# A hybrid decoder trunk on one core: the first load in three pieces, a shorter run of zero products, and the second row tile's products in another order

## Chip, core and metric

The kernel runs on one core of a Trainium2 chip. The metric is the device time of one execution, in microseconds (us). Before the change it is 1411.94 us, the median of three runs (1411.52 to 1412.18).

## What is computed

The reference is a two-layer decoder trunk over 512 tokens of width 1024, all in float32. Layer 0 mixes tokens with a Mamba-2 SSD mixer, layer 1 with HGRN2; each layer then has a layer norm, a squared-ReLU MLP of width 4096, a second layer norm and a gated per-layer input. The change touches only the very beginning, the input projection of the SSD mixer:

```python
def ssd_mixer(u, w_in, conv_w, conv_b, dt_bias, a_log, d_skip, norm_w, w_out):
    zxbcdt = u @ w_in                       # (512 x 1024) @ (1024 x 5152)
    z, xbc, dt = jnp.split(zxbcdt, [SSD_D_INNER, SSD_D_INNER + SSD_CONV_DIM], axis=-1)
    xbc = jax.nn.silu(causal_depthwise_conv(xbc, conv_w, conv_b))
...
def reference(...):
    for i in range(DEPTH):
        mix = ssd_mixer(x, ...) if i % 2 == 0 else hgrn2_mixer(x, ...)
        h = layer_norm(DEEPNORM_ALPHA * x + mix, ...)
        h = layer_norm(DEEPNORM_ALPHA * h + sq_relu_mlp(h, ...), ...)
        x = h + jax.nn.sigmoid(h @ ple_w_gate[i]) * (p[i] @ ple_w_proj[i])
```

## The kernel before

**Products in three parts.** A float32 matrix is taken as a sum of two float32r parts: `hi` is a cast of it (ScalarE, or VectorE in one place), `lo` is the matrix minus `hi` (VectorE). A product of two such matrices is three matmuls, `hi*hi`, `hi*lo` and `lo*hi`, the lines L120, L121 and L122 of the helper `mm3`. They accumulate in one bank of PSUM, [128 x 512].

**The first four columns of blocks.** The activations lie transposed, as eight row tiles of 128 model dimensions by 512 tokens. Each is sent together with the weight rows that meet it (4 blocks of 128 output channels, so also 128 x 512): eight DMAs of 512 KB, L161, one per row tile, issued by SyncE (SP) one after the other into eight slots. The DMA's semaphores are eight lanes used in turn, and a DMA waits until the last one on its lane has landed. For each row tile `k` ScalarE casts the tokens (L167; VectorE for `k = 0`) and the weights (L171), and VectorE makes the two `lo` parts (L168, L172); for `k = 0` the weights are cast in two halves of 256 columns. The four output banks (`py0`, `py1` and two called `pj`) collect the products over `k`:

```python
    with tc.high_priority(offset=FIRST):                                     # L149
        zero = nc.const_aps.tensor(0.0, (P, 1), F32)
        ps = bank(psm, "pm")
        for _ in range(4):
            nc.tensor.matmul(ps[:, :256], zero.to_broadcast([P, P]), zero.to_broadcast([P, 256]), start=True, stop=True)
...
        for k in range(8):
            nc.sync.dma_start(slots[k], a["xw"][k])                          # L161
...
        parts = [[v[:, k % 2, i * P : (i + 1) * P] for v in four[k // 2]] for i in range(4)]
        if k == 0:
            for n, (w, t) in enumerate(((0, x_s.h(k)), (0, x_s.l(k)), (1, x_s.h(k)))):
                for i, out in enumerate(first):
                    nc.tensor.matmul(out, parts[i][w], t, start=n == 0, stop=False)   # L749
        else:
            for i, out in enumerate(first):
                mm3(out, *parts[i], x_s.h(k), x_s.l(k), False, k == 7)
```

For `k = 0` the twelve products go by kind: `hi*hi` of all four banks, then `hi*lo`, then `lo*hi` (L749). From `k = 1` on they go by bank, with `mm3`. In front of everything stand four matmuls of zeros on TensorE, 256 columns each (L153); nothing reads what they write. After `k = 3` come 64 small matmuls for the step sizes (L738), which read all eight slots.

**What follows.** The other blocks of the projection come one at a time, 512 KB of weights each (`unit`, L106 DMA, L113 cast, L116 `lo`), into a bank `pj` with 24 matmuls. Each bank is then convolved over time: ScalarE starts `cv` (L797), VectorE adds three shifted terms (L800: 509, 510 and 511 elements), ScalarE applies SiLU. The scan works on pairs of heads in `core`: TensorE transposes (L859, tile `pt`), VectorE makes from it `xw` and `xdt` (L866, L867), TensorE forms the state products from `xw` (L871, tile `pm`) and the products inside the chunks from `xdt` (L906), VectorE carries the states (L879 to L882, tile `pv`), and TensorE applies them (L923). The decay factors `a` come back from DRAM (L855) and become `b` by VectorE (L888), an exponential on ScalarE (L891) and a product with `cbm` on VectorE (L892).

**What sets the order.** No order is written out by hand here. A list scheduler places the instructions of the whole program when it is built, by priorities and by its own idea of when each would be ready. A change of the first instructions can therefore shift rows that the diff does not name. Each engine then runs its own list strictly in order.

## Time and profile before

| what | value |
|---|---|
| runs before | 1411.52, 1411.94, 1412.18 us |
| the profiled execution | 1411.34 us |
| its span in the trace | 1409.6 us |
| TensorE matmul busy | 1404.3 us (100%) |
| VectorE busy | 1069.1 us (76%) |
| ScalarE busy | 763.6 us (54%) |
| DMA, mean over the span | 129 GB/s |

The profile is of one execution. PE is TensorE's matmuls and PEld its weight loads, DVE is VectorE, ACT is ScalarE, SPq is SyncE's queue. In a timeline a row begins with its start, its duration, the engine and the line; `out<-in` are the tiles; in square brackets stands how long the engine sat idle before it and what it waited for. The chain of waits follows the last instruction backwards, at each step to what released it. Matmuls are pipelined, so the spans of neighbours overlap by some 0.16 us; in the chain the overlap is taken off. Line numbers are those of the kernel before; in the changed kernel those behind L161 are higher by five.

### The profile page before, as it was taken

The page shows a single profiled execution, that of the slowest core. Times are in us where ns is not written, and L with a number is a line of the kernel's source. Part 1 is how long each engine was busy: PE and PEld are TensorE (multiplying, and loading weights), DVE is VectorE, ACT ScalarE, POOL GpSimd, SP SyncE. Part 2 cuts the span into 40 slices and gives each one's busy share as a digit, 9 for nine tenths or more (in the row PEclk, how much of TensorE's full clock was granted, in tenths as well). Part 3 has the DMA queues.
Part 4 walks back from the last instruction along what each step waited for, and adds up shares of the span by engine and source line. Part 5 has one row for each costly group of instructions (what it writes and reads, how often), then busy time and mean ns, then how long its engine had stood idle before and what let it go on. Part 6 is the DMA issues. An engine that isn't in the chain of part 4 may idle for free.

```text
span 1409.6 us, 20400 instructions
## 1 busy us (share of the span) xinstructions
PE 1404.3 (100%) x8001; PEld 1168.1 (83%) x8001; DVE 1069.1 (76%) x1778; ACT 763.6 (54%) x1156; POOL 45.8 (3%) x92
## 2 busy tenths in 40 slices
PE   9999999999999999999999999999999999999998
PEld 7888888888988888888888888888898888888887
DVE  7989688698977668677986577678785867667795
ACT  7766465573354444545555547655555454544573
POOL 0000000001000000000000000000100000000100
PEclk9999999999999999999999999999999999999999
DMA  8433333234433444345621421222443444444731
GB/s 313 135 117 120 106 120 110 85 100 156 141 113 127 157 131 152 129 142 178 209 90 49 134 91 61 76 87 96 150 135 105 147 137 148 144 137 159 202 106 60
DMA packets 50399, 181.69 MB, mean 129 GB/s; under 512 B 5632, under 2 KB 6400, under 8 KB 50176
## 3 DMA queue, kind: packets, MB, share of 16 engines
q1 hardware_dynamic: 38784, 138.45, 29.6%
q0 software_dynamic: 11520, 41.95, 9.2%
q8 instruction: 63, 1.03, 0.3%
q14 instruction: 32, 0.26, 0.1%
HBM read 177.16 MB, written 2.16 MB: 127 GB/s over the span
## 4 chain that ended last, share of the span: by engine, by line
PE 99%; DMA 0%; DVE 0%; issue 0%; DVEq 0%
PE pj L120 25%; PE pj L121 25%; PE pj L122 25%; PE py L120 5%; PE py L122 5%; PE py L121 5%; PE py L906 1%; PE pt L238 1%; PE py L1175 1%; PE pm L923 1%; PE pm L871 1%; PE py L1301 1%; PE pt L859 0%; PE py L1303 0%; PE py L1240 0%; PE py L832 0%
## 5 line engine op out<-in xcount | busy, mean ns | idle before, releaser
L113 ACT CAST whi<-raw 128x1024 fp32r<-128x1024 f32 x218 | 228.8, 1050 | 333.2 <-PE pj L121 243.6
L120 PE MATMUL pj<-b,whi 128*128 128x512 f32 (+1 forms) x990 | 378.6, 383 | 0.0
L122 PE MATMUL pj<-b,wlo 128*128 128x512 f32 (+1 forms) x990 | 376.8, 381 | 0.0
L121 PE MATMUL pj<-b,whi 128*128 128x512 f32 (+1 forms) x990 | 376.6, 381 | 0.0
L116 DVE TENSOR_TENSOR wlo<-raw,whi 128x1024 fp32r<-128x1024 f32 x218 | 265.4, 1221 | 129.4 <-ACT whi L113 128.2
L121 PEld LDWEIGHTS pj<-b,whi 128*128 128x128 f32 x990 | 186.4, 188 | 34.6 <-issue 0.9
L122 PEld LDWEIGHTS pj<-b,wlo 128*128 128x128 f32 x990 | 186.3, 188 | 34.5
L120 PEld LDWEIGHTS pj<-b,whi 128*128 128x128 f32 x990 | 186.1, 188 | 34.0
L122 PE MATMUL pj<-whi,b 128*128 128x512 f32 x520 | 204.1, 392 | 0.0
L120 PE MATMUL pj<-whi,b 128*128 128x512 f32 x508 | 202.1, 398 | 0.0
L121 PE MATMUL pj<-wlo,b 128*128 128x512 f32 x508 | 199.2, 392 | 0.0
L113 ACT CAST whi<-r 128x1024 fp32r<-128x1024 f32 x76 | 80.0, 1053 | 68.5 <-PE pj L122 39.4
L122 PEld LDWEIGHTS pj<-whi,b 128*128 128x128 f32 x520 | 97.7, 188 | 20.1
L120 PEld LDWEIGHTS pj<-whi,b 128*128 128x128 f32 x508 | 95.5, 188 | 19.1 <-ACT b L1322 0.3
L121 PEld LDWEIGHTS pj<-wlo,b 128*128 128x128 f32 x508 | 95.5, 188 | 18.7 <-issue 0.2
L116 DVE TENSOR_TENSOR wlo<-r,whi 128x1024 fp32r<-128x1024 f32 x76 | 92.5, 1220 | 19.6 <-ACT whi L113 19.1
L122 PE MATMUL py<-whi,b 128*128 128x512 f32 x260 | 101.3, 390 | 0.0
L121 PE MATMUL py<-wlo,b 128*128 128x512 f32 x248 | 96.6, 389 | 0.0
L120 PE MATMUL py<-whi,b 128*128 128x512 f32 x248 | 96.4, 390 | 0.0
L329 POOL DMA_DIRECT2D r<-in_w x64 | 34.0, 532 | 1098.8 <-DVE wlo L116 544.3
L122 PEld LDWEIGHTS py<-whi,b 128*128 128x128 f32 x260 | 48.8, 188 | 10.2
L800 DVE SCALAR_TENSOR_TENSOR cv<-pj,cst,cv 128x509 f32<-128x509 f32 (+2 forms) x66 | 48.9, 746 | 10.6 <-ACT cv L797 9.8
(368 smaller groups left out, 1943.5 us busy)
## 6 DMA issues: line engine op xcount, KB each, us to landing
raw<-in_w SPq DMA_DIRECT2D x112, 512.0 KB, 3.3
r<-in_w POOLq DMA_DIRECT2D x64, 512.0 KB, 3.8
raw<-in_wssd SPq DMA_DIRECT2D x36, 512.0 KB, 3.9
a<-csd SPq DMA_DIRECT2D x16, 512.0 KB, 4.1
raw<-in_wso SPq DMA_DIRECT2D x16, 512.0 KB, 3.3
raw<-in_whq SPq DMA_DIRECT2D x16, 512.0 KB, 3.4
raw<-in_wg SPq DMA_DIRECT2D x15, 512.0 KB, 4.0
raw<-in_whvg SPq DMA_DIRECT2D x14, 512.0 KB, 3.4
```

The costliest lines, as they stand in the source:

```text
L113: nc.scalar.copy(hi[:, :n], f)
L116: nc.vector.tensor_sub(lo[:, :n], f, f32(hi[:, :n]))
L120: nc.tensor.matmul(out, sh, mh, start=start, stop=False, **kw)
L121: nc.tensor.matmul(out, sh, ml, start=False, stop=False, **kw)
L122: return nc.tensor.matmul(out, sl, mh, start=False, stop=stop, **kw)
L238: nc.tensor.transpose(pt[:, j * P : (j + 1) * P], src[:, k * P : (k + 1) * P], ident)
L329: queue.dma_start(t[i][u], src)
L800: nc.vector.scalar_tensor_tensor(cv[:, d:], ps[:, : T - d], convw[:, i, k : k + 1], cv[:, d:], ALU.mult, ALU.add)
L871: nc.tensor.matmul(pst_[:, c * P : (c + 1) * P], btok[:, c, :], xw[:, c].rearrange("p h q -> p (h q)"), start=True, stop=True)
L906: mm = nc.tensor.matmul(yds[0][64 * r : 64 * r + 64, sl], xdt[:, 2 * c + r, :], m[:, r, sl], start=True, stop=True)
L923: mm = nc.tensor.matmul(yo[:, c * P : (c + 1) * P], pv[:, c - 1].rearrange("p h q -> p (h q)"), cm[:, c * P : (c + 1) * P], start=True, st ...
L1175: nc.tensor.matmul(pcs[r][bs, at : at + n], kk[r][:, ts], qs, start=True, stop=True)
```

## The change

The fourth matmul of zeros gets 128 columns in place of 256. The first of the eight loads is issued as three DMAs: the tokens (128 x 512), then the weights in two pieces of 128 x 256; the other seven stay as they are. The products of the second row tile (`k = 1`) go by kind, as those of the first do. Casts, subtractions and the number of products stay.

```diff
@@ -149,8 +149,8 @@
-        for _ in range(4):
-            nc.tensor.matmul(ps[:, :256], zero.to_broadcast([P, P]), zero.to_broadcast([P, 256]), start=True, stop=True)
+        for n in (256, 256, 256, P):
+            nc.tensor.matmul(ps[:, :n], zero.to_broadcast([P, P]), zero.to_broadcast([P, n]), start=True, stop=True)
@@ -158,7 +158,12 @@
         for k in range(8):
-            nc.sync.dma_start(slots[k], a["xw"][k])
+            if k == 0:
+                nc.sync.dma_start(slots[0][:, 0, :], a["xw"][0][:, 0, :])
+                for i in range(0, T, 256):
+                    nc.sync.dma_start(slots[0][:, 1, i : i + 256], a["xw"][0][:, 1, i : i + 256])
+            else:
+                nc.sync.dma_start(slots[k], a["xw"][k])
             if k == 3:
@@ -743,10 +748,10 @@
-        if k == 0:
+        if k < 2:
             for n, (w, t) in enumerate(((0, x_s.h(k)), (0, x_s.l(k)), (1, x_s.h(k)))):
                 for i, out in enumerate(first):
-                    nc.tensor.matmul(out, parts[i][w], t, start=n == 0, stop=False)
+                    nc.tensor.matmul(out, parts[i][w], t, start=k == n == 0, stop=False)
```

In the built program the lists of the engines differ at these places, and again in a stretch of the SSD mixer. Behind TensorE's row 310 of some 6290 its list is that of before, row for row. Three places matter.

TensorE, the products of the second row tile (`whi_109` and `wlo_110` its weights, `b_4` the high and `b_6` the low part of the tokens). Before:

```order
L120 MATMUL py_26_174<-b_4_105,whi_109 128x512
L121 MATMUL py_26_174<-b_6_107,whi_109 128x512
L122 MATMUL py_26_174<-b_4_105,wlo_110 128x512
L120 MATMUL py_27_175<-b_4_105,whi_109 128x512
L121 MATMUL py_27_175<-b_6_107,whi_109 128x512
L122 MATMUL py_27_175<-b_4_105,wlo_110 128x512
```

and in the changed kernel:

```order
L754 MATMUL py_26_176<-b_4_105,whi_109 128x512
L754 MATMUL py_27_177<-b_4_105,whi_109 128x512
L754 MATMUL pj_178<-b_4_105,whi_109 128x512
L754 MATMUL pj_179<-b_4_105,whi_109 128x512
L754 MATMUL py_26_176<-b_6_107,whi_109 128x512
L754 MATMUL py_27_177<-b_6_107,whi_109 128x512
L754 MATMUL pj_178<-b_6_107,whi_109 128x512
L754 MATMUL pj_179<-b_6_107,whi_109 128x512
L754 MATMUL py_26_176<-b_4_105,wlo_110 128x512
```

The first product that reads the low weights was the third and is now the ninth.

VectorE, between the convolution of the seventh block (`cv_525` from bank `pj_493`, later `cv_527` from `pj_495`) and the second pair's `xw`. `wlo_759` and `wlo_797` (later `wlo_761`, `wlo_799`) are the low weights of the eleventh and twelfth block; TensorE is in the eighth at that time. Before:

```order
L931 TENSOR_TENSOR ecs_485<-pm_488,ecs_485 128x384
L892 TENSOR_TENSOR b_474<-b_474,cbm_448 128x1024
L888 TENSOR_SCALAR b_588<-a_565,toks_400 128x128 x4
L116 TENSOR_TENSOR wlo_759<-raw_755,whi_757 128x1024
L800 SCALAR_TENSOR_TENSOR cv_525<-pj_493,cst_165,cv_525 128x509
L116 TENSOR_TENSOR wlo_797<-raw_793,whi_795 128x1024
L800 SCALAR_TENSOR_TENSOR cv_525<-pj_493,cst_165,cv_525 128x510
L892 TENSOR_TENSOR b_588<-b_588,cbm_448 128x1024
L800 SCALAR_TENSOR_TENSOR cv_525<-pj_493,cst_165,cv_525 128x511
L866 TENSOR_TENSOR xw_573<-pt_567,toks_400 128x384
```

and in the changed kernel:

```order
L893 TENSOR_SCALAR b_590<-a_567,toks_402 128x128 x5
L805 SCALAR_TENSOR_TENSOR cv_527<-pj_495,cst_167,cv_527 128x509
L936 TENSOR_TENSOR ecs_487<-pm_490,ecs_487 128x384
L805 SCALAR_TENSOR_TENSOR cv_527<-pj_495,cst_167,cv_527 128x510
L897 TENSOR_TENSOR b_590<-b_590,cbm_450 128x1024
L805 SCALAR_TENSOR_TENSOR cv_527<-pj_495,cst_167,cv_527 128x511
L116 TENSOR_TENSOR wlo_761<-raw_757,whi_759 128x1024
L116 TENSOR_TENSOR wlo_799<-raw_795,whi_797 128x1024
L871 TENSOR_TENSOR xw_575<-pt_569,toks_402 128x384
```

Both low-weight subtractions now stand behind the whole convolution; the subtraction `wlo_759` stood ahead of it. `ecs` has moved from ahead of the convolution into it, and the product of `b_474` and `cbm` has moved further ahead.

TensorE, between the transposes `pt` of the second pair and its state products `pm`, which read `xw`. Before:

```order
L859 MATMUL pt_567<-cst_165,xs_389 128x128 x4
L120 MATMUL pj_640<-b_4_105,whi_643 128x512
L121 MATMUL pj_640<-b_6_107,whi_643 128x512
L122 MATMUL pj_640<-b_4_105,wlo_645 128x512
L120 MATMUL pj_640<-b_4_105,whi_643 128x512
L871 MATMUL pm_576<-xw_573,btok_441 128x128 x3
```

and in the changed kernel:

```order
L864 MATMUL pt_569<-cst_167,xs_391 128x128 x4
L120 MATMUL pj_642<-b_4_105,whi_645 128x512
L121 MATMUL pj_642<-b_6_107,whi_645 128x512
L122 MATMUL pj_642<-b_4_105,wlo_647 128x512
L120 MATMUL pj_642<-b_4_105,whi_645 128x512
L121 MATMUL pj_642<-b_6_107,whi_645 128x512
L876 MATMUL pm_578<-xw_575,btok_443 128x128 x3
```

One product more lies between the two.

## Prediction

> **What bounds the kernel now.** I read the chain of waits first, whole and then stretch by stretch, since the page gives TensorE 100% of the span and the question is only what delays TensorE.
>
> ```profile
> PE 99%; DMA 0%; DVE 0%; issue 0%; DVEq 0%
> 0.74 3.40 DMA acc<-in_xw
> 4.17 0.44 DVE b L167
> 4.61 0.14 issue
> 4.74 0.70 PE py L749 x2
> ...
> 1405.12 0.43 DVE sg L456
> ```
>
> From 4.74 us to the last rows on VectorE the chain never leaves TensorE; its 40-us pieces show no other engine. So a product that starts earlier at 4.74 brings the end forward by as much, unless a wait opens on TensorE afterwards, and a wait that opens anywhere costs its full length. That leaves two questions: when the first product starts, and whether the places where the order of VectorE and TensorE has changed open a wait.
>
> Next I read the timeline of the first 5 us.
>
> ```profile
> 0.74 1.80 SPq L161 DMA_DIRECT2D acc<-in_xw  x4
> 0.78 3.36 PE L153 MATMUL pm<-const-float32-0.0 128*128 128x256 f32 x8 [0.78 <-PEq L1452]
> 4.17 0.71 ACT L171 CAST whi<-acc 128x256 fp32r<-128x256 f32 x2 [2.15 <-DMA acc<-in_xw]
> 4.71 0.30 PEld L749 LDWEIGHTS py<-b,whi 128*128 128x128 f32 x2 [0.98 <-ACT whi L171]
> 4.74 0.70 PE L749 MATMUL py<-b,whi 128*128 128x512 f32 x2 [0.61 <-DVE b L167]
> ```
>
> The first tile lands 3.40 us after its issue, at 4.14. Then two things run side by side: VectorE's cast of the tokens (0.44 and 0.14 to the product) and ScalarE's first half of the weights, from 4.17 to the weight load at 4.71, 0.54. Both end within 0.03 us of each other. The zeros keep TensorE until 0.78 + 3.36 = 4.14, so they hold up nothing.
>
> **Term 1, the first load.** The DMA engines move this rate while the first tile arrives (last number of the first row, GB/s; third from its end, 1.00, is the granted clock), and these are the landings of the step weights and of the first four tiles:
>
> ```profile
> 3.50:3.75 0.25, 0.25 (x2) 0.23 (x1) 0.00 (x0) 0.00 (x0) 0.00 (x0) 1.00 1.00 410
> raw<-in_wdt SPq DMA_DIRECT2D x1, 128.0 KB, 6.3
> DMA to landing us min/median/max: 3.4/4.9/6.5
> 2.58 0.58 SPq L164 DMA_DIRECT2D raw<-in_wdt  x1
> ```
>
> At 410 GB/s the tokens' 262 KB take 0.64 us and a piece of weights, 131 KB, 0.32. If the three pieces follow each other at that rate, the last lands at 4.14 as now, the first weights at 4.14 - 0.32 = 3.82, the tokens at 3.50. Small pieces need not lose rate: the step weights, 128 KB in rows as short as those of a piece, were issued at 2.58 and landed 6.3 later, at 8.9; the fourth tile, issued last of four from 0.74 (four issues in 1.80, so 0.45 each, the last at 2.09), landed up to 6.5 later, at 8.6. That is 0.3 us for 128 KB. The weight load then comes 0.03 + 0.54 = 0.57 after 3.82, at 4.39, the product at 4.42; by the tokens it could come at 3.50 + 0.03 + 0.44 + 0.14 = 4.11, which does not decide. The second weight half is cast from 4.21 (0.71 / 2 = 0.36 each), is ready at 4.57 + 0.14 = 4.71, and the third product wants it about 0.5 after 4.42, at 4.9. **Gain 0.32.** The bounds: if the weights came with the tokens, 4.74 - 4.11 = 0.63 gained. If a piece needs from its own issue as long as a whole tile, 3.40, the first weights, issued second at 1.19, land at 4.59 and the product starts at 5.19, 0.45 lost. I take 0.32, since the step weights are the nearest row in size and kind and moved at the full rate.
>
> The Trainium skill, DMA: Bandwidth & Descriptors, section Bandwidth, speaks against cutting a load: it wants at least 1 MiB per DMA for 75% of peak. Here the trace disagrees: 128 KB behind a full queue took 0.3 us, some 0.43 TB/s.
>
> **Term 2, the zeros.** Eight passes take 3.36, so 0.42 each; the change removes half a matmul, one such pass, and the zeros end at 3.72. Since nothing is ready before 4.11 and the product starts at 4.42, the old end, 4.14, would not delay it. 0.
>
> **Term 3, the order of the second row tile.**
>
> ```profile
> 5.43 0.62 ACT L167 CAST b<-acc 128x512 fp32r<-128x512 f32 x1 [0.55 <-DMA acc<-in_xw]
> 6.69 0.68 DVE L172 TENSOR_TENSOR wlo<-acc,whi 128x512 fp32r<-128x512 f32 x1
> 7.59 0.39 PE L120 MATMUL py<-b,whi 128*128 128x512 f32 x1
> 8.04 0.39 PE L122 MATMUL py<-b,wlo 128*128 128x512 f32 x1
> ```
>
> Two more issues of 0.45 move this tile's issue from 1.19 to 2.09; 3.40 after that is 5.49, no later than by 0.1 us, since it lands at 5.4 now, queued behind the first tile. Its low weights are ready at 7.37 and 0.1 later usable. In the old order the third product would want them at 8.04 - 0.32 = 7.72, in the new one the ninth, at 7.27 + 8 x 0.23 = 9.1. Neither waits. A product takes 0.23 in both orders (7.59 to 8.04 is two; the pairs of L749 go in 0.46 in the chain). So 0, but 0.25 us of slack become 1.6. The later issues of SyncE, up to the eighth tile, move by 0.9 us as well and wait for a lane whose piece has long landed; their data queue behind 1.3 us per tile, so that is hidden.
>
> **Term 4, the shifted rows.** The wait that I expect is at the second pair's `xw`, where VectorE's list has changed most. These are the rows of before in time:
>
> ```profile
> 46.73 0.56 DVE L931 TENSOR_TENSOR ecs<-pm,ecs 128x384 f32<-128x384 f32 x1 [0.19 <-PE pm L923]
> 47.20 1.22 DVE L892 TENSOR_TENSOR b<-b,cbm 128x1024 f32<-128x1024 f32 x1
> 49.12 1.22 DVE L116 TENSOR_TENSOR wlo<-raw,whi 128x1024 fp32r<-128x1024 f32 x1
> 50.26 0.75 DVE L800 SCALAR_TENSOR_TENSOR cv<-pj,cst,cv 128x509 f32<-128x509 f32 x1
> 50.93 1.21 DVE L116 TENSOR_TENSOR wlo<-raw,whi 128x1024 fp32r<-128x1024 f32 x1
> 52.06 0.74 DVE L800 SCALAR_TENSOR_TENSOR cv<-pj,cst,cv 128x510 f32<-128x510 f32 x1
> 52.72 1.22 DVE L892 TENSOR_TENSOR b<-b,cbm 128x1024 f32<-128x1024 f32 x1
> 53.85 0.74 DVE L800 SCALAR_TENSOR_TENSOR cv<-pj,cst,cv 128x511 f32<-128x511 f32 x1
> 54.61 0.56 DVE L866 TENSOR_TENSOR xw<-pt,toks 128x384 f32<-128x384 f32 x1
> ```
>
> From start to start: `ecs` 0.47, `cv` 0.67, 0.66 and (without its wait for the transposes) 0.67, the product with `cbm` 1.13, a low-weight subtraction 1.14. On TensorE:
>
> ```profile
> 48.53 0.39 PE L120 MATMUL pj<-b,whi 128*128 128x512 f32 x1
> 53.97 0.60 PE L859 MATMUL pt<-cst,xs 128*128 128x128 f32 x4
> 55.10 0.40 PE L120 MATMUL pj<-b,whi 128*128 128x512 f32 x1
> 55.34 0.83 PE L871 MATMUL pm<-xw,btok 128*128 128x128 f32 x6
> 55.22 0.76 PEld L871 LDWEIGHTS pm<-xw,btok 128*128 128x128 f32 x6 [0.16 <-DVE xw L866]
> 49.46 0.77 ACT L797 ACTIVATE cv<-pj,cst 128x512 f32<-128x512 f32 x1
> ```
>
> All of these would lie 0.32 earlier in the changed kernel; that cancels, so I stay in the time of before. The seventh block's bank is complete when the eighth begins, 48.53 + 0.16 of pipeline = 48.69. ScalarE can start `cv` at 48.79 (it was held by a cast of weights until 49.46), VectorE can follow 0.80 later (49.46 to 50.26), at 49.59. VectorE cannot be the later one: before, it was there at 50.26 after `ecs` and a subtraction that now stand behind, 50.26 - 0.47 - 1.14 = 48.65, with up to 0.9 us for waits of its own. So it sits idle until 49.59, and everything put off comes after: 0.67 + 0.47 + 0.66 + 1.13 + 0.67 + 2 x 1.14 = 5.88, `xw` starts at 55.47. From `xw`'s start to its weight load was 54.61 to 55.22, 0.61, and 0.12 more to the product: 56.20. TensorE wants it one product later than before, at 55.34 + 0.23 = 55.57. **A wait of 0.63.** What follows it, `xdt` for L906, `pv` for L923, keeps its old distance to TensorE. The first pair's `pm` and its `pv` products are moved back by 3 and by 11 products, 0.7 and 2.5 us; the two steps now ahead of `pv` on VectorE cost 1.13 + 1.14 = 2.3, which fits inside 2.5. The bounds: 0 if VectorE needs less than I count, and 1.9 if ScalarE's `cv` is held by the row just ahead of it, an exponential on the next pair's `a`, whose load was issued at 45.82:
>
> ```profile
> 45.82 3.78 SPq L855 DMA_DIRECT2D a<-csd  x2
> a<-csd SPq DMA_DIRECT2D x2, 512.0 KB, 4.1
> ```
>
> Landing 4.1 later, at 49.92, it would let `cv` start near 50.1, 1.3 later than 48.79. I do not take that: the load waits for readers of its buffer, and they stand earlier now.
>
> **Sum.** -0.32 + 0 + 0 + 0.63 = +0.31. The profiled execution took 1411.34 (span 1409.60, 1.74 around it) and would take 1411.65; it lies 0.60 under the median of the three runs, and the median becomes 1411.94 + 0.31 = 1412.25, **1412.2**.
>
> **The rivals.**
>
> *No wait opens.* The scheduler put one more product ahead of L871, and TensorE waited nowhere before. Then -0.32 alone stays: 1411.6, with 0.63 gained at the bound 1411.3. Against it: in the trace `xw` was already only 0.16 ahead of being late at the weight load.
>
> *The load is not earlier.* The pieces cost their own issue and latency, the product starts at 5.19: +0.45 + 0.63, 1413.0. For it: 3.40 us for the first tile holds far more than the 1.28 that 524 KB take at 410 GB/s. Against it: the latencies of queued loads overlap, as the step weights show.
>
> *`cv` is held by the load of `a`*: -0.32 + 1.9, 1413.5.
>
> *The clock, on the slow side.* The zeros run slowly: 0.42 per 256 columns is 1.64 ns a column, while float32 matmuls later,
>
> ```profile
> 40.48 0.89 PE py L832 x8
> ```
>
> take 0.11 per 128 columns, 0.87 ns. The granted clock reads 1.00 in both, so the pace tells more. By 4.74 the pace is full. If fewer zeros leave TensorE at half pace when the products begin, they lose half of the time until the pace doubles: with a stretch as long as the zeros, 3.4 us, up to 1.7 us, on average 0.85: 1413.1. It makes the kernel slower by over 0.2% (2.82 us) from the point at which half pace lasts 2 x (2.82 - 0.31) = 5.0 us past the first product. Against it: the zeros end 0.42 earlier but the product starts 0.32 earlier, so the gap, 0.6 before, grows only to 0.7.
>
> The Trainium skill, TensorE: Matmul & The Clock Gate, section Part 1: The HAM clock gate (the "warmup" mystery), says that TensorE starts at half clock and is let go after about 3.4 us of sustained work, counted in windows that run on whatever the kernel does. The doubled pace in this trace agrees; by that rule 2.98 us of zeros could miss a window that 3.36 us met, at the price above.
>
> **How the numbers follow.** My forecast 0.52, no wait 0.25, the clock 0.10, load not earlier 0.08, `cv` held 0.05. The range must take in 1411.3 below and the load's 1413.0 and the clock's mean 1413.1 above; 1413.3 leaves out the clock's longer half and the held `cv`, about 1 in 10, and little below. A measurement of this kernel can tell about 0.2%, 2.8 us, from no change. No case with its price reaches that in either direction, save the clock's tail beyond 5 us: slower 0.03, faster 0.01 for what I have not seen, within 0.2% 0.96.
>
> **What would show it.** Right: tokens cast near 3.5, first product near 4.4; VectorE idle for about a microsecond ahead of the seventh block's first shifted term, and a weight load of the second `pm` that waits 0.6 for `xw`; from there a chain on TensorE alone. Wrong: a first product at 4.7 or later (term 1), products of 0.45 in the first microseconds (the clock), no wait at `pm` (term 4), or a wait at L923 of the first pair, which I held to be covered.

## The result, and the profile after

The changed kernel takes **1414.68 us**, median of 22 runs (1412.55 to 1415.84); the kernel before took 1411.95 us beside it, also 22 runs (1411.25 to 1415.32). The ratio is **1.0016**, 95% interval 1.0009 to 1.0023: 2.7 us slower where the prediction had 0.3. The profiled execution took 1414.27 us, its span is 1412.5.

The chain of waits of the changed kernel, first 60 us (start, duration, what; in order of time):

```profile
2.11 6.16 DMA acc<-in_xw
8.30 0.62 ACT b L172
8.91 0.53 ACT whi L176
9.49 0.73 PE py L754 x2
...
46.63 3.79 DMA a<-csd
50.74 0.68 ACT cv L802
51.44 0.75 DVE cv L805
...
57.28 0.56 DVE xw L871
57.89 0.94 PE pm L876 x6
```

Before, the chain went over to TensorE at 4.74 us and stayed there. Now it does so only at 9.49, because it waits for the load of the *second* row tile, and it leaves TensorE once more, between 42 and 58 us, for the shifted rows. Those are two places. The first is read in the timeline of TensorE:

```profile
4.30 1.03 PE L754 MATMUL py<-b,whi 128*128 128x512 f32 x2 [0.20 <-ACT whi L176]
5.78 0.73 PE L754 MATMUL pj<-b,whi 128*128 128x512 f32 x2 [0.45 <-ACT whi L176]
...
7.73 0.61 PE L754 MATMUL pj<-b,wlo 128*128 128x512 f32 x2
9.49 0.73 PE L754 MATMUL py<-b,whi 128*128 128x512 f32 x2 [1.15 <-ACT whi L176]
```

The first product does start earlier, at 4.30 instead of 4.74. But two waits follow (the numbers in brackets), 0.45 us for the second piece of weights and 1.15 us for the second tile, and the first pair of products is slow (1.03 where the pair before took 0.70; why is told under rest_only). The thirteenth product, with which the second tile begins, starts at 9.49 where it started at 7.59: **1.90 us late**. From the first product to the thirteenth 5.19 us pass where 2.85 did; 1.30 of these 2.34 us more lie directly ahead of the thirteenth. The casts on ScalarE show what the waits wait for:

```profile
3.84 0.40 ACT L176 CAST whi<-acc 128x256 fp32r<-128x256 f32 x1 [1.82 <-DMA acc<-in_xw]
5.33 0.40 ACT L176 CAST whi<-acc 128x256 fp32r<-128x256 f32 x1 [1.08 <-DMA acc<-in_xw]
8.30 0.62 ACT L172 CAST b<-acc 128x512 fp32r<-128x512 f32 x1 [2.57 <-DMA acc<-in_xw]
```

The first piece is there at 3.84, close to what the prediction worked out (3.85); the second is cast at 5.33 where the prediction had 4.21, and the second tile's tokens at 8.30 where the kernel before had 5.43. The view by stretches gives the reason (last number: GB/s; the number before it: busy share of the DMA engines). Before:

```profile
3.00:3.50 0.50, 0.50 (x3) 0.37 (x2) 0.00 (x0) 0.00 (x0) 0.00 (x0) 1.00 0.97 393
3.50:4.00 0.50, 0.50 (x3) 0.23 (x1) 0.00 (x0) 0.00 (x0) 0.00 (x0) 1.00 1.00 410
4.00:4.50 0.50, 0.13 (x1) 0.00 (x0) 0.33 (x1) 0.33 (x2) 0.00 (x0) 1.00 1.01 410
4.50:5.00 0.50, 0.26 (x1) 0.29 (x2) 0.47 (x2) 0.38 (x2) 0.00 (x0) 1.00 1.00 328
```

and after:

```profile
3.00:3.50 0.50, 0.50 (x3) 0.37 (x2) 0.00 (x0) 0.00 (x0) 0.00 (x0) 1.00 0.97 240
3.50:4.00 0.50, 0.50 (x3) 0.31 (x1) 0.46 (x2) 0.16 (x1) 0.00 (x0) 1.00 1.25 162
4.00:4.50 0.50, 0.30 (x2) 0.20 (x2) 0.50 (x1) 0.25 (x1) 0.00 (x0) 1.00 0.46 131
4.50:5.00 0.50, 0.50 (x2) 0.30 (x2) 0.50 (x2) 0.00 (x0) 0.00 (x0) 1.00 0.77 287
```

For two microseconds the engines move 131 to 287 GB/s instead of about 400. They move 0.41 MB in this time instead of 0.77, and 0.36 MB at 400 GB/s is 0.9 us. I call this stretch **the hole** below. The busy share does not fall with the rate: in the first of the two microseconds it stands at 0.97 and 1.25, so packets were under way and took longer (packets of 4 KB that began between 3.5 and 4.0 us took 0.40 us in the median, before 0.16). It is not all of the 2.9 us by which the second tile is late: a tile has landed when the last of the 16 engines has finished its part, and in a list of the packets 15 engines were done with the second tile at 6.59 and one at 8.28.

The second place, the second pair's state products:

```profile
50.52 0.22 ACT L881 ACTIVATE cd<-a 128x8 f32<-128x8 f32 x1 [1.65 <-DMA a<-csd]
50.65 0.76 ACT L802 ACTIVATE cv<-pj,cst 128x512 f32<-128x512 f32 x1
51.44 0.75 DVE L805 SCALAR_TENSOR_TENSOR cv<-pj,cst,cv 128x509 f32<-128x509 f32 x1 [0.82 <-ACT cv L802]
57.89 0.74 PEld L876 LDWEIGHTS pm<-xw,btok 128*128 128x128 f32 x6 [0.53 <-DVE xw L871]
```

VectorE sits idle for 0.82 us ahead of the seventh block's first shifted term, and the weight load of the second `pm` waits 0.53 us for `xw`. The prediction had 1 and 0.63.

### The profile page after: what moved, and what is told of

Its sections match the earlier page's. It is cut to its first block, busy times and chain, and to the rows that moved or that the text cites. A ratio compares the mean times of both kernels' runs of the same rounds, so it can differ in the third digit from the quotient of the medians.

```text
span 1412.5 us, 20394 instructions
## 1 busy us (share of the span) xinstructions
PE 1405.6 (100%) x8001; PEld 1168.4 (83%) x8001; DVE 1068.9 (76%) x1778; ACT 764.3 (54%) x1156; POOL 45.8 (3%) x92
## 3 DMA queue, kind: packets, MB, share of 16 engines
q8 instruction: 63, 1.03, 0.3%
## 4 chain that ended last, share of the span: by engine, by line
PE 98%; DMA 1%; DVE 1%; ACT 0%; SPq 0%; issue 0%; ACTq 0%; DVEq 0%
PE pj L120 25%; PE pj L121 25%; PE pj L122 24%; PE py L120 5%; PE py L121 5%; PE py L122 5%; PE py L911 1%; PE pt L243 1%; PE py L1180 1%; PE pm L876 1%; PE pm L928 1%; PE py L1306 1%; DMA acc<-in_xw 0%; PE pt L864 0%; PE py L1308 0%; PE py L1245 0%
```

## The experiments

**How they are read.** One run varies by more than the effects sought (the kernel before: 124 runs, 1411.25 to 1415.32), so beside the medians I use each kernel's trace, and in it three distances from the trace of before, n-th matmul against n-th matmul: at the thirteenth product (7.59 us before; "head"), from there to the matmul at 100 us ("rows"), and from there to the last matmul ("rest").

| kernel | median, lowest to highest (runs) | profiled | 1st product | 13th | head | rows | rest |
|---|---|---|---|---|---|---|---|
| before | 1412.19, 1411.25 to 1415.32 (124) | 1411.34 | 4.74 | 7.59 | 0 | 0 | 0 |
| after | 1414.68, 1412.55 to 1415.84 (22) | 1414.27 | 4.30 | 9.49 | +1.90 | +0.51 | +0.11 |
| cut_only | 1413.48, 1411.61 to 1414.22 (11) | 1412.38 | 4.64 | 7.53 | -0.06 | +0.45 | +0.63 |
| rest_only | 1413.17, 1411.25 to 1415.34 (11) | 1413.62 | 4.74 | 9.76 | +2.18 | +0.08 | +0.01 |
| order_only | 1413.82, 1411.84 to 1415.03 (11) | 1415.03 | 4.71 | 9.71 | +2.12 | +0.41 | +0.69 |
| split_only | 1414.07, 1413.73 to 1415.95 (11) | 1414.58 | 4.34 | 10.02 | +2.43 | +0.39 | +0.05 |
| three_old_order | 1416.36, 1415.81 to 1418.42 (5) | 1416.36 | 7.08 | 11.49 | +3.90 | 0.00 | +0.73 |
| zeros3 | 1413.45, 1411.65 to 1414.31 (11) | 1414.04 | 4.65 | 9.39 | +1.80 | +0.83 | +0.06 |
| zeros45 | 1413.06, 1411.99 to 1413.77 (11) | 1413.34 | 4.61 | 8.23 | +0.65 | -0.01 | +1.33 |
| zeros5 | 1412.49, 1412.00 to 1413.55 (11) | 1412.30 | 4.82 | 8.05 | +0.47 | +0.03 | +0.43 |
| two_parts | 1414.23, 1412.73 to 1415.75 (11) | 1414.23 | 5.00 | 9.92 | +2.33 | +0.01 | +0.11 |
| packed | 1414.10, 1413.04 to 1415.58 (11) | 1413.94 | 4.30 | 9.15 | +1.56 | +0.63 | +0.05 |
| act_second | 1415.25, 1413.50 to 1416.48 (11) | 1416.30 | 6.21 | 10.99 | +3.40 | 0.00 | +1.18 |
| after_zeros5 | 1414.10, 1413.17 to 1415.33 (11) | 1413.73 | 4.82 | 8.77 | +1.18 | +0.18 | +0.65 |
| later_split | one run | 1412.79 | 4.90 | 8.20 | +0.61 | +0.03 | +0.43 |
| first_alone | one run | 1412.43 | 4.53 | 8.09 | +0.50 | +0.11 | +0.10 |
| late_cast | one run | 1417.49 | 6.33 | 11.60 | +4.01 | +1.33 | +0.18 |

My first theory was that all 2 us of the head were late loads. The first four experiments, one part of the change each, made it fall.

### rest_only: the change without the cut load

```diff
-        for _ in range(4):            # zeros, 256 columns each
+        for n in (256, 256, 256, P):
-        if k == 0:                    # L746, the products by kind
+        if k < 2:
```

> The shorter zeros and the new order of the second row tile, with the first load whole; the later rows then stand as in the kernel before. Theory 'load' (cutting the first tile makes the second tile land about 2 us late, and the shifted rows add 0.5): nothing of either is in this kernel, so 1411.9, within 0.3 of the kernel before, first product at 4.7, second tile cast at 5.4. Rival 'clock' (the shorter zeros leave TensorE at half pace): about 0.9 slower, 1412.8, with products of 0.45 us behind 4.7.

Measured: ratio 1.0006 (0.9997 to 1.0015), and a wide spread. The load is whole and lands as before (cast of the second tile's tokens at 5.4 us), yet in the profiled run the thirteenth product is 2.18 us late. The timeline of TensorE says why:

```profile
4.74 1.19 PE L749 MATMUL py<-b,whi 128*128 128x512 f32 x2 [0.64 <-DVE b L167]
5.73 1.05 PE L749 MATMUL pj<-b,whi 128*128 128x512 f32 x2
6.58 1.05 PE L749 MATMUL py<-b,whi 128*128 128x512 f32 x2
...
9.14 0.78 PE L749 MATMUL pj<-b,wlo 128*128 128x512 f32 x2
9.76 0.62 PE L749 MATMUL py<-b,whi 128*128 128x512 f32 x2
```

From start to start two products take 0.85 us (5.73 to 6.58), 0.43 each, where before they took 0.23; from 9.76 on they take 0.23. **The first eleven products run at half pace**, without any wait. It is the rival that the prediction called the clock, at more than its highest price.

### order_only: the whole load, with the later rows of the changed kernel

An extra load of 64 KB that nobody reads, behind the eighth tile, brings the scheduler to the same later order as in the changed kernel; with it only the load of the first tile differs from the changed kernel.

```diff
 # as rest_only, and in the loop over the eight tiles:
+            if k == 7:
+                nc.sync.dma_start(dtw[:, 256:384], a["wdt"][:, :128])
```

> The first load whole, one more load of 64 KB behind the eighth tile that nothing reads; with it the later rows stand exactly as in the changed kernel. Theory 'load': only the wait at the second pair's xw is left, 0.5 to 0.6 slower than before, 1412.5; the weight load of the second pm waits about 0.5 us. Rival 'order' (the shifted rows cost all of it): 2.5 slower, 1414.5. A third possibility, that the wait is not there with the load whole: 1411.9.

Measured: 1.0009 (1.0000 to 1.0018). Again half pace (13th product at 9.71), and besides the wait at the second `pm`:

```profile
58.00 0.74 PEld L874 LDWEIGHTS pm<-xw,btok 128*128 128x128 f32 x6 [0.54 <-DVE xw L869]
```

In rest_only the same weight load waits 0.21 us for `xw`. The two differ by 0.65 us in the median, 0.59 in the lowest run and 0.33 in the column "rows". So the shifted rows cost some 0.3 to 0.65 us with the whole load as well. The wait at the second `pm` is the firmer sign of it, since each of the two kernels varies by 3 to 4 us over its eleven runs. The old rows are not free of waits either: in cut_only and zeros3, which have them, the "rows" of 0.45 and 0.83 come from the first pair's `pm`, which waits for its `xw` near 43 to 45 us.

### split_only: the cut load alone

```diff
-            nc.sync.dma_start(slots[k], a["xw"][k])
+            # k == 0: tokens, then two pieces of weights, as in the change
```

The four old zeros and the old order of the second tile's products stay; the later rows fall as in the changed kernel.

> The three loads of the change, with the old zeros and the old order of the second row tile; later rows as in the changed kernel. Theory 'load': as the changed kernel, 1414.5, second tile cast near 8 us; the new order of the products neither helps nor hurts, since all four of the second tile's parts come late together. Rival 'clock' or 'order of the products': the loss goes, 1412.

Measured: 1.0014 (1.0005 to 1.0023); no run below 1413.73. The hole is there (158 GB/s at 3.5 to 4.0), the second tile lands at 7.5, and since the products run at half pace until 9.7, with the four whole zeros in front of them, its lateness hides behind them: the second tile's first product, at 10.02, waits for nothing. Half pace and a late tile do not add up; the longer one counts. Its lowest run lies 1.2 above that of the changed kernel, which has the new order of the second tile's products. That fits a late second tile, whose low weights are wanted third in the old order and ninth in the new one, but I did not test it apart.

### three_old_order: pieces of 128 and 384 columns, later rows as before

```diff
-                for i in range(0, T, 256):
+                for i, j in ((0, 128), (128, 512)):
```

> Three loads for the first tile, but weights cut at column 128 instead of 256 (pieces of 512 bytes and 1.5 KB a row); with this the later rows stand as in the kernel before. Theory 'load': the second tile lands late by about 2, and without the wait at xw the total is 2.0 slower, 1414.0. Rival 'order': 0.4 faster than before, 1411.5.

Measured: 1.0033 (1.0020 to 1.0046), by a mishap of its own. ScalarE's table load came to stand behind the wait for the first cast's weights, which here lie in both pieces (1.28 us, from 5.33 to 6.6), and the first product starts at 7.08. For the sum of the times it is lost, apart from the column "rows", 0.00: with the later rows of before no wait opens at the second `pm`. But it is the one trace that shows the granted clock low (third number from the end):

```profile
6.00:7.00 1.00, 0.00 (x0) 0.00 (x0) 0.00 (x0) 0.99 (x3) 0.00 (x0) 1.00 0.97 360
8.00:9.00 1.00, 1.00 (x4) 0.71 (x4) 0.25 (x1) 0.90 (x2) 0.00 (x0) 0.50 1.05 400
```

By the trace's records the clock is 1.00 from 3.62 us, during the zeros, 0.50 from 7.03, after TensorE has sat idle for 3.15 us, and 1.00 again from 10.44; the three times lie 3.41 us apart. The products take 0.43 us in the stretch at 0.50 and 0.23 after it. So half pace is the clock at one half.

### cut_only: half a matmul of zeros less, nothing else

```diff
-        for _ in range(4):
+        for n in (256, 256, 256, P):
```

> Before with the fourth matmul of zeros cut to 128 columns and nothing else changed; all other rows as before. Theory A (the pace): some runs that would have doubled their pace ahead of the first product now keep 0.43 per product until 8 to 10 us; fastest runs stay at 1411.3, slowest reach 1415, median 1412.7 to 1413.4. Rival (the 128 columns less cost nothing, as the prediction has it): median and range of before, 1412.0 to 1412.5.

Measured: median 1413.48, ratio 1.0004 (0.9995 to 1.0013). The runs fall in two groups: five from 1411.61 to 1412.38 and six from 1413.48 to 1414.22. The profiled one belongs to the lower group and is at full pace from the second product on:

```profile
4.64 0.76 PE L749 MATMUL py<-b,whi 128*128 128x512 f32 x2 [0.54 <-DVE b L167]
5.23 0.62 PE L749 MATMUL pj<-b,whi 128*128 128x512 f32 x2
```

The same program head gave half pace until 9.5 us in rest_only and order_only and full pace here; whether it does is a matter of the run. What the cut seems to change is how often. Over 1413 us lie 22 of the 124 runs of before (18%), and 12 of the 22 runs of cut_only and rest_only, which differ from before in the head by the zeros and, in rest_only, by the order of the second tile's products. The median is 0.8 to 1.3 higher, though each ratio's interval still reaches 1. The count is a rough sign, since a run can be long for other reasons: zeros45 and zeros5 (below), whose traces come to full pace early, have 6 and 3 of 11 runs over 1413. And four whole zeros do not assure the pace: in the three traces that have them it doubled at 3.60 us (before), 5.86 (later_split) and 9.66 (split_only).

### zeros3: one whole matmul of zeros less

```diff
-        for _ in range(4):
+        for _ in range(3):
```

> Before with three matmuls of zeros (256 columns each) instead of four; nothing else differs, and every later row of every engine is that of before. The zeros end near 3.3 us (six passes of 0.43), the first product still starts at 4.74. Theory A (the pace): TensorE's pace doubles only after a stretch of some 3.4 us in which it was mostly busy, and such stretches lie differently in each run; with 1.4 us idle ahead of the first product, the stretch must begin behind it in most runs, so products of 0.43 last until 7.6 to 11 us: median 1413.0 to 1414.3, slowest runs near 1414.5, few runs at 1411.3. Rival (the spread of the runs has nothing to do with the zeros): the median stays that of before, about 1412.3, with runs from 1411.3 to 1414.

Measured: median 1413.45, ratio 1.0007 (0.9998 to 1.0016), 7 of 11 runs over 1413. The zeros end at 3.68 by the trace, TensorE is idle for 0.97 us, and the products are at half pace:

```profile
0.78 2.90 PE L153 MATMUL pm<-const-float32-0.0 128*128 128x256 f32 x6 [0.78 <-PEq L1452]
4.65 1.19 PE L749 MATMUL py<-b,whi 128*128 128x512 f32 x2 [0.97 <-DVE b L167]
...
8.92 0.63 PE L749 MATMUL pj<-b,wlo 128*128 128x512 f32 x2
```

As expected from the pace; that as many as three runs stay below 1412.2 was not.

### zeros5 and zeros45: more zeros

```diff
-        for _ in range(4):
+        for _ in range(5):                     # zeros5
+        for n in (256, 256, 256, 256, P):      # zeros45
```

> Before with five matmuls of zeros instead of four; nothing else differs. The zeros reach 4.6 to 5.1 us, so TensorE never sits idle ahead of the first product, which starts at 4.6 to 5.1. Theory A (the pace): the pace doubles at the latest near 7 us in every run; products of 0.43 last 2 us at most, the first product is up to 0.3 late: fastest runs 1411.3 to 1411.6, slowest near 1412.8, median 1411.6 to 1412.2, a smaller spread than that of before. Rival (the spread has nothing to do with the zeros): median that of before or 0.3 above, runs up to 1414 as before.

> Before with four whole matmuls of zeros and a fifth of 128 columns; nothing else differs. The zeros reach 4.3 to 4.55 us, so the idle stretch ahead of the first product falls from 0.6 to 0.2 to 0.4 and the product is not held up. Theory A (the pace): the pace doubles by 7 us in every run, and in a third of them before the first product: median 1411.4 to 1412.0, slowest near 1412.8; below before. Rival: as before, or as with five matmuls of zeros, 1412.2 to 1412.6.

Measured: zeros5 median 1412.49, 1.0004 (0.9995 to 1.0013), none over 1413.55; zeros45 median 1413.06, 1.0005 (0.9996 to 1.0013), none over 1413.77. In both traces the pace doubles early, at 5.5 and 6.3 us: in zeros5

```profile
4.82 1.12 PE L749 MATMUL py<-b,whi 128*128 128x512 f32 x2
5.78 0.62 PE L749 MATMUL pj<-b,whi 128*128 128x512 f32 x2
```

so the head is late by only 0.47 and 0.65, and the spread is smaller than that of before. But the medians did not come below that of before, as the pace alone would have it, and in zeros45 that expectation failed outright. Part of the reason stands in the column "rest": the profiled run of zeros45 loses 1.33 us far from the head, at one place, where TensorE waits for a sum on VectorE:

```profile
701.91 0.39 PE L121 MATMUL pj<-wlo,a 128*128 128x512 f32 x1
703.42 0.50 PE L120 MATMUL py<-whi,a 128*128 128x512 f32 x1 [1.13 <-DVE lnsum L373]
```

Act_second shows the same wait, the others little or none of it. So there is a second lottery at 702 us, and I found no version that beats both kernels.

### two_parts and packed: fewer pieces, and pieces without stride

```diff
 # two_parts: the weights in one piece; later rows as before
-                for i in range(0, T, 256):
-                    nc.sync.dma_start(slots[0][:, 1, i : i + 256], a["xw"][0][:, 1, i : i + 256])
+                nc.sync.dma_start(slots[0][:, 1, :], a["xw"][0][:, 1, :])
 # packed: tokens and both pieces each from a DRAM array of its own; rows as in the change
+                nc.sync.dma_start(slots[0][:, 0, :], a["x0"])
+                    nc.sync.dma_start(slots[0][:, 1, i : i + 256], a["w0%d" % (i // 256)])
```

> The first tile as two DMAs: tokens (128 x 512), then the weights whole (128 x 512); the shorter zeros and the new order of the second tile's products as in the changed kernel; all later rows of the engines those of before (so no wait at the second pair's state product). Theory B1 (the hole in the DMA rate at 3 to 5 us comes with the number of small loads at the head of an empty queue): half of the hole, tokens cast at 3.5, weights at 4.2, first product 4.7 to 4.8, second tile cast near 6. Theory B2 (it comes from the pieces' rows of 1 KB): no hole, second tile cast at 5.4 to 5.5. By both the products of the second tile start by 8 or are hidden, and the median is 1412.3 to 1413.5, that of the version with the whole load (1413.2) within the spread that the pace makes. If it costs as much as three pieces, second tile at 8 and fastest runs above 1412.3.

> The changed kernel with tokens and the two pieces of weights each in a DRAM array of its own, so that a piece is read from one stretch of 128 KB instead of 1 KB rows 4 KB apart; all rows of the engines as in the changed kernel. If the strided rows make the hole (theory B2): the rate stays near 400 GB/s, third piece cast by 4.4, second tile by 5.6, fastest runs 1.0 to 1.5 below those of the changed kernel (1412.55), near 1411.5 with the 0.5 of the shifted rows in it. If the number and smallness of the loads make it (theory B1): second piece cast near 5.3, second tile landed at 7 to 8.3, times of the changed kernel (1412.5 to 1415.8, median 1414.7).

Measured: two_parts 1.0014 (1.0006 to 1.0023), packed 1.0014 (1.0005 to 1.0023). Neither closes the hole. With two loads:

```profile
3.50:4.00 0.50, 0.50 (x3) 0.30 (x1) 0.45 (x2) 0.00 (x0) 0.00 (x0) 1.00 0.68 131
4.00:4.50 0.50, 0.10 (x1) 0.00 (x0) 0.50 (x1) 0.00 (x0) 0.00 (x0) 1.00 0.82 160
```

the second tile is cast at 7.76, and in packed, with 57 and 100 GB/s in the same stretches, at 7.96. So neither the stride in DRAM (packed has none) nor the pieces' rows of 1 KB (two_parts has rows of 2 KB) are needed for it, and the number of pieces hardly matters either: what I had expected, half of the hole with two loads and none without the stride, was wrong both times. Packed, whose products came to full pace within the first pair, shows what the load costs by itself: 13th product at 9.15, 1.56 late.

### later_split, first_alone, late_cast: where the hole comes from

```diff
 # later_split: before, with another tile cut
+            if k == 5:    # instead of k == 0: tokens, then two pieces
 # first_alone: whole first tile, then two loads of 64 KB that nobody reads
+                nc.sync.dma_start(slots[0], a["xw"][0])
+                for i in range(2):
+                    nc.sync.dma_start(dtw[:, 256 + 128 * i : 384 + 128 * i], a["wdt"][:, 128 * i : 128 * i + 128])
 # late_cast: the change; the first casts take a factor of one made from the last piece
+                nc.vector.tensor_scalar(late, slots[0][:, 1, 254:258], 0.0, 1.0, ALU.mult, ALU.add)
```

> Before, with the sixth of the eight tiles (not the first) loaded as tokens and two pieces of weights; four tiles stand ahead of it in the queue, so the DMA engines have bytes to move all the time. Rows of all engines but SyncE as before. If the hole in the rate comes from too few bytes in the queue (theory B1), or from the casts that begin when the first tokens land (theory B3): no hole, the rate stays near 390 to 420 GB/s from 3 to 11 us, time 1411.3 to 1413.3 as before. If loads of such pieces are slow wherever they stand: the rate falls below 300 GB/s for a microsecond near 9 to 11 us, and the seventh and eighth tile land 1 to 2 us later.

> Whole first tile, then two extra loads of 64 KB (rows of 512 bytes, read by nobody) ahead of the second tile; shorter zeros and the new order of the second tile's products as in the changed kernel. The second tile is issued at 2.1 us as in the changed kernel, but nothing lands before the first tile at 4.14. Theory B1 (hole because little lies in the queue): 650 KB are ahead of the second tile until 4.45, its descriptors are long there: no hole, second tile cast at 5.7. If the number of loads issued ahead makes it: hole from 3.2 to 5, first tile after 4.5, second at 7 to 8. Theory B3 (casts): no hole before 4.14.

> The changed kernel, but the first casts of VectorE and ScalarE take a factor of one that VectorE works out from both pieces of weights, so neither engine begins before the last piece has landed; the result is the same, the first product is later by up to a microsecond. Theory B3 (the hole comes from the casts, which begin at 3.5 while loads still flow): no hole from 3.2 to 4.5, last piece at 3.9 to 4.2, second tile at 5.5. Theory B1 (the loads themselves): hole as in the changed kernel, last piece at 5.3, second tile at 7.5 to 8.3.

Measured, in the same stretches of half a microsecond: later_split (its own three pieces go between 9.5 and 11 us, at 281, 395 and 420 GB/s, and the eighth tile is cast at 14.05, before at 14.09):

```profile
3.50:4.00 0.50, 0.50 (x3) 0.31 (x1) 0.00 (x0) 0.00 (x0) 0.00 (x0) 1.00 1.07 426
4.00:4.50 0.50, 0.50 (x2) 0.00 (x0) 0.17 (x1) 0.17 (x1) 0.00 (x0) 1.00 1.01 401
```

first_alone:

```profile
3.50:4.00 0.50, 0.50 (x3) 0.30 (x1) 0.04 (x1) 0.04 (x1) 0.00 (x0) 1.00 1.34 232
4.00:4.50 0.50, 0.10 (x1) 0.00 (x1) 0.47 (x2) 0.50 (x2) 0.00 (x0) 1.00 0.74 120
```

late_cast:

```profile
3.50:4.00 0.50, 0.50 (x3) 0.31 (x1) 0.00 (x0) 0.17 (x1) 0.00 (x0) 1.00 1.02 102
4.00:4.50 0.50, 0.10 (x1) 0.00 (x0) 0.00 (x0) 0.50 (x1) 0.00 (x0) 1.00 1.19 102
```

Late_cast has the hole though no cast begins before 5.5, so the early casts are not the cause. Later_split has none: the same three pieces behind four whole tiles delay nothing. First_alone has it with a whole first tile, when two small loads stand between it and the second; it was expected to have none if "little lies in the queue" were the reason, so that reason, in the form in which I had put it, fell as well. What the kernels with a hole share is the issue of the second tile: at 1.65 us or later in all of them, at 1.2 in those without.

### act_second: the second tile issued early, the pieces kept

```diff
-                nc.sync.dma_start(slots[k], a["xw"][k])
+                (nc.scalar if k == 1 else nc.sync).dma_start(slots[k], a["xw"][k])
```

> The changed kernel with the second tile loaded from ScalarE's queue at 0.74 us instead of from SyncE's behind the three pieces; rows of the second pair of the mixer move again. Theory B1 (the three pieces and the second tile are issued more slowly than the DMA engines move them, and engines that have run out of descriptors are slow to go on): with 1 MB issued by 1.2 us there is no hole, the rate stays near 400 from 3.0 to 4.5, last piece at 4.5 at the latest, second tile cast before 5.6, products of the second tile by 7.6 at full pace; first product 4.5 to 5.0, since the pieces share the engines with the second tile. Median 1412.0 to 1413.5 (the shorter zeros and up to 0.5 of shifted rows in it). If pieces at the head cost by themselves: hole again, second tile cast after 6.8.

Measured: 1.0018 (1.0009 to 1.0027). The hole is gone, with all three pieces in place:

```profile
0.74 0.41 ACTq L166 DMA_DIRECT2D acc<-in_xw  x1
0.74 0.39 SPq L162 DMA_DIRECT2D acc<-in_xw  x1
```

```profile
3.50:4.00 0.50, 0.50 (x3) 0.31 (x1) 0.00 (x0) 0.00 (x0) 0.00 (x0) 1.00 1.04 422
4.00:4.50 0.50, 0.10 (x1) 0.00 (x0) 0.00 (x0) 0.00 (x0) 0.00 (x0) 1.00 0.90 359
```

That agrees with an issue that falls behind, but does not show it, since the second tile here has another queue as well as an earlier issue. One issue takes 0.45 us: a whole tile of 524 KB is issued at 1165 GB/s, a piece of 131 KB at 290, and the engines move about 400. What it does not explain is that the rate falls to 100 to 160 and not just to 290, that the engines stay busy with slow packets meanwhile, and that in the changed kernel one engine ends 1.7 us after the others. Where the hole comes from stays open; that loads of less than a whole tile ahead of the second tile, in the same queue, bring it is what the runs show. As a repair it is no use. The four loads share the engines and their data begin later (61 GB/s in the half microsecond from 2.0), so the tokens are cast at 5.20 and the first product starts at 6.21, where I had said 4.5 to 5.0. Until the pieces are there TensorE is idle for 2.1 us, and then it is at half pace.

### after_zeros5: the changed kernel with more zeros

```diff
-        for n in (256, 256, 256, P):
+        for _ in range(5):
```

> The changed kernel with five matmuls of zeros of 256 columns (its own four are 256, 256, 256, 128); all other rows as in the changed kernel. The zeros end at 4.6 to 5.1, up to 0.7 later than the first weights are there. Theory: the pace doubles by 7 us in each run, so what is left beside zeros5 (1412.5) is the late second tile (products of the second tile at 8.8 to 9.5 instead of 8.05) and the shifted rows (0.5): median 1413.4 to 1414.4, spread under 2 us, against 1412.5 to 1415.8 in the changed kernel. If the pace has no part in the changed kernel's loss: median 1414.7 to 1415.2, spread 3 us.

Measured: 1.0014 (1.0005 to 1.0023), spread 2.2 us (I had expected less than 2). The median is 1.6 above that of zeros5, which has the same zeros, the whole load and the old rows. That is the price of load and shifted rows with the zeros made alike; 0.6 below the changed kernel, it also lies where I had expected it. The trace does not show that price: of its 1.18 - 0.47 = 0.71 in the head the pace made nearly all, since it doubled at 6.95 us and in zeros5 at 5.45. The second tile was cast at 6.86 in this one run, in that of the changed kernel at 8.30, and its first product, at 8.77, waits for nothing.

## Why the prediction was wrong, point by point

**The step that failed is Term 1, with its continuation in Term 3:** "Small pieces need not lose rate", and the second tile lands "no later than by 0.1 us". The first half of the term was right: tokens cast at 3.51 (worked out: 3.53), first weights at 3.84 (3.85), first product at 4.30 (4.42). The second half was not. The row that I leant on, the step weights, is a load of 128 KB *behind four whole tiles*, and there a cut load costs nothing (later_split). At the head of an empty queue the rate fell to 131 to 287 GB/s for two microseconds: the second piece was cast at 5.33 instead of 4.21, and most of the price falls on the second tile, which I moved by two issues of 0.45 and found "no later"; it was cast at 8.30 instead of 5.43. In the profiled run these are the waits of 0.45 and 1.15; without slow products (packed) the head is 1.56 late. The upper bound of the term, 0.45 lost, looked at the first product alone and so missed the place of the loss. That the change stays within 0.2%, to which I gave 0.96, came true with 0.16%, but by the width of that limit and not by the sum: the median lies above the price of every rival (1413.5 at most).

The Trainium skill, DMA: Bandwidth & Descriptors, section Bandwidth, wants at least 1 MiB per DMA; I set that aside on the strength of the same row. The runs agree with neither reading as it stands: such pieces went at 281 to 420 GB/s behind four tiles; at the head the engines moved 283 to 365 GB/s from 2.0 to 3.0 us (changed kernel) and 57 to 287 in the hole (packed and changed kernel).

**Term 2, the zeros, was put at 0 and is not.** I asked whether the zeros hold up the first product, which they don't. What they do is to bring the pace up. I read 0.42 us for each of the eight passes of zeros; in the trace of before the second to the seventh start 0.43 apart, but the pace doubled in the seventh, at 3.60. Where it did not, the same zeros took 3.75 us in place of 3.36 (split_only, later_split). So the shorter ones of the changed kernel, at half pace, ended at 4.11 and not at 3.72. Nor did the granted clock read 1.00 while the zeros were slow: the trace has no record of it before 3.60. The rival that I named for this ("the clock") had a chance of 0.10 and an average price of 0.85. Its half pace is real (rest_only, zeros3), its price is up to 2.2 us, and it is no either-or: split_only has it with the four whole zeros. How often it strikes is known only by the counts over 1413 us (18% of the runs of before, about half of those with fewer zeros); that the long runs of before are such runs is not shown, as only one of them all was traced. My bound on its length, a stretch as long as the zeros, 3.4 us, was too short: half pace lasted 4.8 us past the first product.

The Trainium skill, TensorE: Matmul & The Clock Gate, section Part 1: The HAM clock gate (the "warmup" mystery), says that the activity window runs freely and that the same kernel shows different numbers of slow matmuls from run to run. The traces agree: the pace had doubled by the second product in cut_only and only at the twelfth in rest_only and order_only, with the same zeros and the same load.

**Term 3, the order,** cost nothing and helped a little where the second tile was late: in the changed kernel the low weights are ready at 10.25 and wanted at 11.43.

**Term 4, the shifted rows, was right** in place and nearly in size: 0.53 us at the second `pm` for 0.63, with VectorE idle ahead of `cv`. What held `cv` was the load of `a`, as in the rival that I had given 0.05 (ScalarE waited 1.65 us for it, up to 50.52), but with TensorE already 1.9 us late there was little left to lose by it. So the size is in part luck: each trace with the changed kernel's rows has a head that is late by 1.2 us or more, and what the load of `a` would cost behind a punctual one is open. The 0.16 us that I read as what `xw` had to spare in the kernel before was a wait of the weight load already.

**Sum.** Put together from the medians: the zeros (rest_only) +0.8, the shifted rows (order_only less rest_only) +0.65, the cut load (after less order_only) +0.9, in all 2.3; the rest to the 2.7 measured is the difference between the medians of before that were taken beside them (1412.35 and 1411.95). The shares depend on the order in which the parts are taken, as half pace and a late tile do not add up: split_only, the cut load with its rows and the old zeros, is alone 1.7 slower. The cut load's share is smaller here than the 1.6 of packed, since a late tile costs nothing while the products run at half pace.

## What to carry to other kernels

- A price read from a load in a full queue does not hold at the head of an empty one. Compare the bytes issued per microsecond (here 131 KB in 0.45 us) with what the engines move, as a warning though not as a proven cause, and follow the *next* load, not only the one that was cut.
- Work that seems to do nothing may be what keeps an engine at its pace. Before trimming it, look at the duration of the first instructions behind it in more than one execution.
- Where runs vary by more than the effect, compare traces stretch by stretch, matmul by matmul: the same 2 us at the head can be late data in one run and a slow pace in the next.

## What the runs showed of the hardware

- The view's granted clock reads 1.00 also where products take 0.43 us instead of 0.23, as long as the trace has no record of the clock. The first record comes when the pace doubles: at 3.60 us in before, 4.75 in cut_only, 4.99 in the changed kernel, 9.47 in rest_only. Where there is a record (three_old_order), half pace reads 0.50. In front of the first record the pace is seen in the durations only.
- The traces of the variants differ in at least three places besides the loads: the pace in the first ten microseconds (0 to 2.2 us), the waits for `xw` near 43 to 58 us (0 to 0.8), and a wait for VectorE's sum at 702 us (0 to 1.3). They are likely sources of the spread of the kernel before, 4 us in 1412, of which there is one trace only.
- SyncE's issues grew longer towards the end of the hole: 0.71 and 1.01 us for the fifth and sixth tile in the changed kernel, 0.46 and 0.45 before. Whether slow issue makes the hole or both have one cause is not settled.

```profile
4.01 0.71 SPq L166 DMA_DIRECT2D a<-in_xw  x1
4.76 1.01 SPq L166 DMA_DIRECT2D b<-in_xw  x1
```
